# Sums of squares for the q and k norms from ScalarE's accumulator, head by head, instead of ScalarE's squares and VectorE's sums

## The chip, the cores and the metric

The kernel runs on one core of one Trainium2 chip. The metric is the device time in microseconds, as the median of several runs; lower is better.

## The reference, cut to what matters

A decoder trunk of two layers over 512 positions of width 1024, in float32. Layer 0 has an mLSTM group and a sparse-attention group (NSA: 8 query heads of 64 columns, 2 groups of keys and values); layer 1 is a gated linear recurrence (HGRN2). The change touches the norms and rotary turns of the NSA's queries, selected keys and window keys:

```python
def rms_norm(x, w):
    xf = x.astype(jnp.float32)
    return xf * lax.rsqrt(jnp.mean(xf * xf, axis=-1, keepdims=True) + EPS) * w.astype(jnp.float32)
...
    qh = partial_rope(rms_norm(heads(q, NSA_HEADS), q_norm), pos) * (d ** -0.5)
...
    ks_h = partial_rope(rms_norm(heads(ks, G), k_norm[1]), pos)
...
    kw_h = partial_rope(rms_norm(heads(kw, G), k_norm[2]), pos)
```

The mean runs over the 64 columns of one head, so a tile of 128 positions needs 8 sums for q, and 4 for k (2 groups, selected and window).

## The kernel before, in words

**Work.** All dense products run as three fp32r matmuls of a high and a low part. A weight tile comes in by DMA (`raw`), ScalarE rounds it (`whi`) and VectorE takes the rest (`wlo`). Layer 0 projects in groups: `cg` (compression inputs and gates), `nq` (queries), `nkv` (keys and values), `nz` (the gate z, called the z weights below), `mq`, `mk`, `mv`, `mo`, `mz`, then the output projection; layer 1 follows. A group's products go to PSUM buffers `mm`, and its evacuation on VectorE adds the bias and puts them in SBUF.

**The norms.** `nq_evac` and `nkv_evac` (lines 1175 to 1191) write the q and k columns of a 128-token tile to `qk` and start `prep_q(i)` or `prep_k(i)` (lines 1210 to 1269), once for each of the four tiles. A prep squares the tile on ScalarE into a buffer `sq`, multiplies the norm's weights in on GpSimd (`qk<-qk,qnB` or `knB`), sums the squares of each head on VectorE (`qss`, `kss`), takes the mean and the power -0.5 on GpSimd (`rsqrt_mean`, line 710: `qrs`, `krs`), multiplies on VectorE (`x<-qk,qrs` or `x<-qk,krs`), turns the first 16 columns (`rot`, three VectorE instructions with `r`), and lets TensorE transpose the result (`tp<-cs,x`). ScalarE and VectorE split the transposed tile into two parts (`q`, `kd`). With q of a tile and the compressed keys `kcd` the compressed scores follow (`sc<-kcd,q`, `ce`), and with all tiles of q and k the selected and window scores (`sc<-kd,q`).

**Beside it.** Between 30 and 55 us the gates of the mLSTM (`rows`, `ML`, `bd`) and the compressed keys (`gb`: a small product, a tanh on ScalarE that needs a table load, a transpose, another small product, giving `kr`, `kn`, `kh`, `kcd`) run beside the dense `nq` and `nkv` products.

**Order.** No engine's order is written out by hand. Generators (`Flow`) record the work, and a planner (`Plan.schedule`, lines 284 to 390) sets each engine's order from due times and from a price for each instruction (`price`, line 517); it is emitted at line 408, so nearly all instructions bear that line, and they are told apart by their tiles. Layer 0 and layer 1 are planned one after the other. Each engine then takes its queue in order. PSUM buffers for transposes (`tp`) are two, `mm` three; the raw weights have three buffers, the split ones four; the large scratch buffers `big` (which held `sq`) five.

ScalarE's accumulator is used in the kernel before too: by the mLSTM's head norms (`hj<-nd,rd`), by layer 1's (`hj<-tq`), by the compressed keys' norm (`kn<-kr`), and by the exponentials of the attention (`PP`). An instruction that reads the accumulator out, ACTIVATION_READ_ACCUMULATOR, stands behind each of them in the trace.

Of the kernel before, what the change touches and what calls it, by code (L numbers as in the profile page):

```python
# [16 lines left out]
AF = mybir.ActivationFunctionType  # L17
OP = mybir.AluOpType
AX = mybir.AxisListType
# [128 lines left out]
def cust(ap, dims, off=0):  # L148
    return bass.AP(tensor=ap.tensor, offset=ap.offset + off,
                   ap=[list(ap.ap[0])] + [list(d) for d in dims])  # L150
# [465 lines left out]
def build(tc, I, out):  # L616
    nc = tc.nc
    fl, pl = Flow(), Plan()
    V, A, P = (Paced(fl, e, n, pl) for e, n in ((nc.vector, "V"), (nc.scalar, "A"), (nc.gpsimd, "P")))
# [3 lines left out]
    with ExitStack() as ctx:  # L623
# [42 lines left out]
        def cut(t, shape, p=slice(0, 128)):  # L666
            n = 1
            for d in shape:
                n *= d
            v = t[p, :n]  # L670
            if len(shape) == 1:
                return v
            ls = "abcdef"[:len(shape)]
            return v.rearrange("p (" + " ".join(ls) + ") -> p " + " ".join(ls), **dict(zip(ls, shape)))
# [7 lines left out]
        def has(n):  # L682
            return lambda: room[0] >= n

        def u_t(name, shape, dt=F32):
            room[0] -= 1
            assert room[0] >= 0, name
            return cut(up.tile([128, 2064], dt, name=name, tag="u"), shape)

        def u_end(n):  # L690
            room[0] += n
# [18 lines left out]
        def rsqrt_mean(o, ss, n, inv, p=128):  # L710
            P.tensor_scalar(o, ss, inv, EPS, op0=OP.mult, op1=OP.add)
            P.tensor_tensor(o, o, hm[:p, :n], op=OP.pow)
# [234 lines left out]
        with ExitStack() as c0:  # L947
# [3 lines left out]
            def s_t(name, shape, bufs=2, dt=F32):  # L951
                return sp.tile(shape, dt, name=name, tag=name, bufs=bufs)
# [3 lines left out]
            def hb(n):  # L956
                return lambda: big[0] >= n

            def b_end(n=1):
                big[0] += n  # L960

            def b_t(name, shape, dt=F32):
                big[0] -= 1
                assert big[0] >= 0, name
                return cut(sp.tile([128, 1280], dt, name=name, tag="big", bufs=BB), shape)
# [24 lines left out]
            def E(n):  # L990
                return ev.setdefault(n, Mark())
# [183 lines left out]
            def nq_evac(i, p):  # L1175
                if i % 2 == 0:
                    t = u_t("qk", (2, 12, 64))
                    qk[i], qk[i + 1] = t[:, 0], t[:, 1]
                V.scalar_tensor_tensor(flat(qk[i][:, :8, :]), p, rs[:, i:i + 1], st["bq"], op0=OP.mult, op1=OP.add)
                fl.add(prep_q(i), 1)  # L1180


            def nkv_evac(i, p):
                if i == 0:
                    st["bk"] = bias_t("nkv", 512)
                    t = u_t("vp", (2, 1024))
                    st["vall"], st["pcT"] = cut(t[:, 0], (4, 4, 64)), cut(t[:, 1], (2, 512))
                bk = st["bk"]
                V.scalar_tensor_tensor(flat(qk[i][:, 8:, :]), p[:, :256], rs[:, i:i + 1], bk[:, :256], op0=OP.mult, op1=OP.add)
                V.scalar_tensor_tensor(flat(st["vall"][:, i]), p[:, 256:], rs[:, i:i + 1], bk[:, 256:], op0=OP.mult, op1=OP.add)  # L1190
                fl.add(prep_k(i), 1)
# [3 lines left out]
            def rot(x2, i):  # L1195
                r1 = s_t("r1", [128, 8, 16], 2)
                V.tensor_tensor(r1.rearrange("p a (c d) -> p a c d", c=2),
                                cust(x2, [[64, 8], [-8, 2], [1, 8]], 8),
                                cust(cs, [[0, 8], [8, 2], [1, 8]], SC["sin"] + 16 * i), op=OP.mult)
                V.tensor_tensor(x2[:, :, :16], x2[:, :, :16], cust(cs, [[0, 8], [1, 16]], SC["cos"] + 16 * i),  # L1200
                                op=OP.mult)
                V.tensor_tensor(x2[:, :, :16], x2[:, :, :16], r1, op=OP.add)

            def turn(x2):
                p = tp_t()
                for c in range(4):
                    T.transpose(p[:, 128 * c:128 * (c + 1)], flat(x2[:, 2 * c:2 * c + 2]), idf)
                return cut(p, (4, 128))

            def prep_q(i):  # L1210
                yield hb(2)
                x = qk[i][:, :8, :]
                ts_ = slice(128 * i, 128 * (i + 1))
                sq = b_t("sq", (8, 64))
                A.activation(sq, x, AF.Square)
                P.tensor_tensor(x, x, cust(qnB, [[0, 8], [1, 64]]), op=OP.mult)
                ss = s_t("qss", [128, 8])
                V.tensor_reduce(ss, sq, axis=AX.X, op=OP.add)
                b_end()
                rq = s_t("qrs", [128, 8])  # L1220
                rsqrt_mean(rq, ss, 8, 1.0 / 64)
                x2 = b_t("x2", (8, 64))
                V.tensor_tensor(x2, x, cust(rq, [[1, 8], [0, 64]]), op=OP.mult)
                rot(x2, i)
                yield [None, TPS, (lambda: q2) if i else has(2)]
                if i == 0:
                    q2.extend(u_t("q2", (2, 2, 512), F32R) for _ in range(2))
                p4 = turn(x2)
                b_end()
                for o in range(2):  # L1230
                    a, b = slice(64 * o, 64 * o + 64), slice(64 - 64 * o, 128 - 64 * o)
                    for g in range(2):
                        pg = p4[a, 2 * g:2 * g + 2]
                        A.activation(q2[g][a, o, :, ts_], pg, AF.Copy)
                        V.tensor_tensor(q2[g][b, o, :, ts_], pg, q2[g][a, o, :, ts_].bitcast(F32), op=OP.subtract)
                fl.mark(E("q%d" % i))
                fl.add(cmp_sm(i), 2)

            def prep_k(i):
                yield hb(2)  # L1240
                x = qk[i][:, 8:, :]
                ts_ = slice(128 * i, 128 * (i + 1))
                sq = b_t("sq", (4, 64))
                A.activation(sq, x, AF.Square)
                P.tensor_tensor(x.rearrange("p (a b) c -> p a b c", a=2), x.rearrange("p (a b) c -> p a b c", a=2),
                                cust(knB, [[64, 2], [0, 2], [1, 64]], 64), op=OP.mult)
                ss = s_t("kss4", [128, 4])
                V.tensor_reduce(ss, sq, axis=AX.X, op=OP.add)
                b_end()
                rk = s_t("krs4", [128, 4])  # L1250
                rsqrt_mean(rk, ss, 4, 1.0 / 64)
                x2 = b_t("x2", (8, 64))
                V.tensor_tensor(x2.rearrange("p (a b) c -> p a b c", a=4), cust(qk[i], [[64, 4], [0, 2], [1, 64]], 512),
                                cust(rk, [[1, 4], [0, 2], [0, 64]]), op=OP.mult)
                rot(x2, i)
                yield [None, TPS, (lambda: kd) if i else has(2)]
                if i == 0:
                    kd.extend(u_t("kd", (2, 2, 512), F32R) for _ in range(2))
                p4 = turn(x2)
                b_end()  # L1260
                for g in range(2):
                    pg = p4.rearrange("p (b g) t -> p g b t", b=2)[:, g]
                    A.activation(kd[g][:, 0, :, ts_], pg, AF.Copy)
                    V.tensor_tensor(kd[g][:, 1, :, ts_], pg, kd[g][:, 0, :, ts_].bitcast(F32), op=OP.subtract)
                fl.mark(E("k%d" % i))
                if i == 3:
                    u_end(2)
                    fl.add(nsa_a(), 0)
                    fl.add(nsa_b(), 0)
# [448 lines left out]
        with ExitStack() as c1:  # L1718
# [23 lines left out]
            for j in range(2):  # L1742
                a = s_t(f"AL{j}", [128, 4, 32], 1)
# [375 lines left out]
```

## Time and profile before

| | |
|---|---|
| runs | 623.8, 623.28, 620.89 us; median 623.28 |
| profiled execution | 619.54 us |
| its span, first to last instruction | 617.8 us |
| busy: TensorE, weight loads | 609.2 us (99%), 492.0 us (80%) |
| busy: VectorE, ScalarE, GpSimd | 463.9 us (75%), 326.4 us (53%), 104.5 us (17%) |
| mean granted TensorE clock | 0.997 of full |

The names are those of the profile: PE is TensorE's matmuls, PEld its weight loads, DVE VectorE, ACT ScalarE, POOL GpSimd, SP SyncE. Matmuls overlap one another, so the distance between two starts says what one costs, not its duration; the same holds for short ACT and DVE instructions. A busy PE may still run slower than it could.

### The profile page before, as it was taken

The numbers are of one execution on the slowest core, as the hardware profiler recorded it, in microseconds if no ns is written. First come the engines' busy times: TensorE is split into PE (matmuls) and PEld (weight loads), VectorE is DVE, ScalarE is ACT, GpSimd is POOL, SyncE is SP. The second block draws the span as 40 slices with busy tenths as digits, with TensorE's granted clock in tenths as the row PEclk, the third lists the DMA queues.
The fourth block names the chain that finished last, engine by engine and source line by source line (L and its number), as shares of the span: only waits on it lengthen the run. The fifth ranks groups of instructions, "written<-read, shape, count | busy, mean of one in ns | idle before, by whom it ended". The sixth has DMA issues, their size and how long they took to land.

```text
span 617.8 us, 11670 instructions
## 1 busy us (share of the span) xinstructions
PE 609.2 (99%) x4498; PEld 492.0 (80%) x4498; DVE 463.9 (75%) x988; ACT 326.4 (53%) x778; POOL 104.5 (17%) x131
## 2 busy tenths in 40 slices
PE   8999998999999999999999999999999999999997
PEld 8877886877777777888888887788877877788886
DVE  5888989988899875656746669997688798986441
ACT  7554433675676765273534757447527375565410
POOL 1424252031100000063003111023000100122100
PEclk9998999999999999999999999999999999999999
DMA  8823137679994004016244424473222215473111
GB/s 293 278 117 103 51 103 256 203 164 342 247 203 138 0 2 147 7 46 228 77 162 136 154 85 138 118 240 121 69 72 69 70 34 173 138 282 128 35 69 68
DMA packets 23526, 82.90 MB, mean 134 GB/s; under 512 B 3376, under 2 KB 4272, under 8 KB 20656
## 3 DMA queue, kind: packets, MB, share of 16 engines
q1 hardware_dynamic: 21168, 65.39, 32.2%
q0 software_dynamic: 2304, 16.78, 10.3%
q8 instruction: 35, 0.57, 0.4%
q14 instruction: 19, 0.16, 0.1%
HBM read 77.96 MB, written 20.97 MB: 160 GB/s over the span
## 4 chain that ended last, share of the span: by engine, by line
PE 92%; DVE 3%; DMA 1%; issue 1%; POOL 1%; ACT 1%; SPq 0%; ACTq 0%; DVEq 0%
PE mm L408 35%; PE mx L408 17%; PE my L408 15%; PE sc L408 8%; PE tp L408 5%; PE ac L408 5%; PE tq L408 5%; PE sd L408 2%; DMA raw<-in_wall_dram 1%; DVE wlo L408 1%; DVE HB L408 0%; DVE AL L408 0%; POOL krs L408 0%; ACT whi L408 0%; DVE x L408 0%
## 5 line engine op out<-in xcount | busy, mean ns | idle before, releaser
L408 ACT ACTIVATE whi<-raw 128x512 fp32r<-128x512 f32 (+1 forms) x184 | 105.0, 614 | 76.2 <-PE my L408 29.5
L408 DVE TENSOR_TENSOR wlo<-raw,whi 128x1024 fp32r<-128x1024 f32 (+1 forms) x96 | 114.7, 1202 | 20.4 <-ACT whi L408 20.1
L408 PE MATMUL mm<-whi,h0h 128*128 128x512 f32 (+1 forms) x168 | 68.2, 407 | 0.0
L408 PE MATMUL mm<-whi,h0l 128*128 128x512 f32 (+1 forms) x168 | 67.9, 405 | 0.0
L408 PE MATMUL mm<-wlo,h0h 128*128 128x512 f32 (+1 forms) x168 | 67.4, 405 | 0.0
L408 ACT ACTIVATE PP<-sc,nm 128x128 f32<-128x128 f32 (+2 forms) x64 | 33.7, 527 | 26.0 <-DVE nm L408 22.9
L408 DVE CUSTOM_DVE_ANT_0 sc<-sc,cz 128x128 f32<-128x128 f32 (+2 forms) x64 | 31.4, 502 | 11.7 <-PE sc L408 9.1
L408 PE MATMUL mm<-h0h,whi 128*128 128x512 f32 x96 | 39.5, 411 | 0.0
L408 PE MATMUL mm<-h0h,wlo 128*128 128x512 f32 x96 | 38.1, 397 | 0.6 <-DVE wlo L408 0.6
L408 PE MATMUL mm<-h0l,whi 128*128 128x512 f32 x96 | 38.6, 402 | 0.0
L408 PEld LDWEIGHTS mm<-whi,h0l 128*128 128x128 f32 x168 | 32.1, 192 | 5.8 <-issue 0.2
L408 PEld LDWEIGHTS mm<-wlo,h0h 128*128 128x128 f32 x168 | 32.2, 192 | 5.6 <-issue 0.2
L408 PEld LDWEIGHTS mm<-whi,h0h 128*128 128x128 f32 x168 | 32.3, 192 | 5.2
L408 DVE TENSOR_TENSOR HB<-HB,tt 128x512 f32<-128x512 f32 x48 | 31.9, 687 | 4.4 <-PE sd L408 3.1
L408 PE MATMUL sc<-kd,q 128*128 128x512 f32 (+3 forms) x128 | 31.3, 330 | 0.0
L408 ACT ACTIVATE PT<-tp 128x384 f32<-128x384 f32 (+1 forms) x48 | 24.0, 526 | 9.5 <-PE tp L408 9.2
L408 POOL TENSOR_TENSOR ivgg<-ivgg,zz 128x256 f32<-128x256 f32 x16 | 17.8, 1116 | 65.9 <-ACT zz L408 65.9
L408 POOL TENSOR_SCALAR hr<-hs 128x4 f32<-128x4 f32 x12 | 2.3, 193 | 142.7 <-ACT hj L408 142.6
L408 PE MATMUL tp<-cs,PP 128*128 128x128 f32 x160 | 26.3, 275 | 0.0
L408 PEld LDWEIGHTS sc<-kd,q 128*128 128x128 f32 x128 | 22.7, 191 | 4.0 <-ACT PT L408 0.8
L408 PE MATMUL my<-h1l,whi 128*128 128x512 f32 x64 | 25.8, 403 | 0.0
L408 PE MATMUL mx<-h1l,whi 128*128 128x512 f32 x64 | 25.8, 402 | 0.0
(374 smaller groups left out, 1556.7 us busy)
## 6 DMA issues: line engine op xcount, KB each, us to landing
raw<-in_wall_dram SPq DMA_DIRECT2D x76, 512.0 KB, 3.8
wt<-in_wall_dram POOLq DMA_DIRECT2D x12, 1024.0 KB, 14.2
raw<-wt SPq DMA_DIRECT2D x16, 512.0 KB, 3.7
wt<-wt POOLq DMA_DIRECT2D x4, 1024.0 KB, 22.7
bias<-in_brow_dram SPq DMA_DIRECT2D x9, 256.0 KB, 4.1
xt<-in_xt_dram SPq DMA_DIRECT2D x8, 256.0 KB, 5.4
w<-in_cw_dram SPq DMA_DIRECT2D x2, 1024.0 KB, 9.4
x<-in_xt_dram SPq DMA_DIRECT2D x2, 1024.0 KB, 6.8
```

Of the source, the lines that this page charges most:

```text
L408: o.fn(*o.a, **k)
```

## The change

A helper `squares` calls one ScalarE activation for each head, with 64 columns in and a scratch tile out, and lets the accumulator write the head's sum. The buffer `sq`, the full-width square and VectorE's `tensor_reduce` go, and a prep waits for one large scratch buffer instead of two. What follows, from `rsqrt_mean` on, is the same code.

```diff
+            def squares(x, ss):
+
+                j = cut(s_t("sqj", [128, 512], 1), (8, 64))
+                for a in range(x.shape[1]):
+                    A.activation(j[:, a, :], x[:, a, :], AF.Square, accum_out=ss[:, a:a + 1])
+
             def prep_q(i):
-                yield hb(2)
+                yield hb(1)
                 x = qk[i][:, :8, :]
                 ts_ = slice(128 * i, 128 * (i + 1))
-                sq = b_t("sq", (8, 64))
-                A.activation(sq, x, AF.Square)
+                ss = s_t("qss", [128, 8])
+                squares(x, ss)
                 P.tensor_tensor(x, x, cust(qnB, [[0, 8], [1, 64]]), op=OP.mult)
-                ss = s_t("qss", [128, 8])
-                V.tensor_reduce(ss, sq, axis=AX.X, op=OP.add)
-                b_end()
...
             def prep_k(i):
-                yield hb(2)
+                yield hb(1)
                 x = qk[i][:, 8:, :]
                 ts_ = slice(128 * i, 128 * (i + 1))
-                sq = b_t("sq", (4, 64))
-                A.activation(sq, x, AF.Square)
+                ss = s_t("kss4", [128, 4])
+                squares(x, ss)
...
-                ss = s_t("kss4", [128, 4])
-                V.tensor_reduce(ss, sq, axis=AX.X, op=OP.add)
-                b_end()
```

The planner then sets another order for the first layer. Two places of it matter. The first is ScalarE's queue around the table load for the tanh of the compressed keys (`gb`); `cT` are the compression inputs, `qk_174` holds q tiles 0 and 1. Before:

```order
L408 ACTIVATE cT_152<-tp_157 64x64x8
L408 ACTIVATE sq_175<-qk_174 128x512
L408 ACT_TABLE_LOAD
L408 ACTIVATE gb_161<-gb_161 128x128
L408 ACTIVATE whi_180<-raw_170 128x512 x2
L408 ACTIVATE gb_161<-tp_173 128x64
L408 ACTIVATE sq_182<-qk_174 128x512
```

With the change:

```order
L408 ACTIVATE cT_152<-tp_157 64x64x8
L408 ACTIVATE sqj_176,qss_175<-qk_174 128x64 x8
L408 ACTIVATE sqj_183,qss_182<-qk_174 128x64 x8
L408 ACT_TABLE_LOAD
L408 ACTIVATE gb_161<-gb_161 128x128
L408 ACTIVATE gb_161<-tp_173 128x64
L408 ACTIVATE whi_180<-raw_170 128x512 x2
```

The squares of both tiles now stand ahead of the table load, and the first weight split has moved behind `gb`.

The second is VectorE's queue at the last two splits of the z weights: `wlo_260` and `wlo_268` before, `wlo_263` and `wlo_271` with the change; `x2_264` and `x2_267` are k tile 2. Before:

```order
L408 SCALAR_TENSOR_TENSOR vp_232<-mm_249,rs0_89,bias_231 128x256
L408 TENSOR_REDUCE kss4_262<-sq_261 128x4
L408 TENSOR_TENSOR wlo_260<-raw_230,whi_259 128x1024
L408 SCALAR_TENSOR_TENSOR qk_206<-mm_251,rs0_89,bias_231 128x256
L408 TENSOR_TENSOR x2_264<-qk_206,krs4_263 128x512
L408 TENSOR_TENSOR wlo_268<-raw_266,whi_267 128x1024
L408 TENSOR_REDUCE kss4_270<-sq_269 128x4
L408 TENSOR_TENSOR r1_265<-x2_264,cs_68 128x128
L408 TENSOR_TENSOR x2_264<-x2_264,cs_68 128x8x16
L408 TENSOR_TENSOR x2_264<-x2_264,r1_265 128x8x16
L408 TENSOR_TENSOR kd_275<-tp_277,kd_275 128x2x128
```

With the change:

```order
L408 SCALAR_TENSOR_TENSOR qk_205<-mm_250,rs0_89,bias_230 128x256
L408 SCALAR_TENSOR_TENSOR vp_231<-mm_250,rs0_89,bias_230 128x256
L408 TENSOR_TENSOR wlo_263<-raw_225,whi_262 128x1024
L408 TENSOR_TENSOR wlo_271<-raw_269,whi_270 128x1024
L408 TENSOR_REDUCE ce_256<-sc_255 128x256
L408 TENSOR_TENSOR x2_267<-qk_205,krs4_266 128x512
L408 TENSOR_REDUCE mx8_257<-ce_256 128x8
L408 SCALAR_TENSOR_TENSOR qk_205<-mm_251,rs0_89,bias_230 128x256
L408 TENSOR_TENSOR ce_256<-ce_256,mx8_257 128x256
L408 TENSOR_TENSOR r1_268<-x2_267,cs_68 128x128
L408 TENSOR_TENSOR x2_267<-x2_267,cs_68 128x8x16
```

Both weight splits have moved ahead of the multiplication of k tile 2, and work on the compressed scores (`ce`, `mx8`) of an earlier tile stands between the steps of k tile 2.

## Rows read from the trace of the kernel before

**Rows 1.** The page, part 1: busy time, share of the span, instructions.
```profile
PE 609.2 (99%) x4498; PEld 492.0 (80%) x4498; DVE 463.9 (75%) x988; ACT 326.4 (53%) x778; POOL 104.5 (17%) x131
```
**Rows 2.** Windows: length, busy of PE, PEld, DVE, ACT, POOL; PE clock, DMA share, GB/s.
```profile
80.00:100.00 20.00, 18.16 (x91) 14.34 (x90) 17.94 (x40) 6.14 (x16) 8.22 (x11) 1.00 0.57 196
```
**Rows 3.** Timeline of PE around 94 us: start, duration, engine, what, [idle before, releaser].
```profile
92.83 0.40 PE L408 MATMUL mm<-h0h,whi 128*128 128x512 f32 x1
93.07 0.39 PE L408 MATMUL mm<-h0l,whi 128*128 128x512 f32 x1
94.05 0.50 PE L408 MATMUL mm<-h0h,wlo 128*128 128x512 f32 x1 [0.59 <-DVE wlo L408]
94.39 0.39 PE L408 MATMUL mm<-h0h,whi 128*128 128x512 f32 x1
95.99 0.63 PE L408 MATMUL tp<-cs,x 128*128 128x128 f32 x4 [1.21 <-DVE kd L408]
```
**Rows 4.** Timeline of DVE in the same stretch.
```profile
91.40 0.69 DVE L408 TENSOR_TENSOR x<-qk,krs 128x512 f32<-128x512 f32 x1 [1.48 <-POOL qk L408]
92.01 1.98 DVE L408 TENSOR_TENSOR wlo<-raw,whi 128x1024 fp32r<-128x1024 f32 x1
...
95.09 0.75 DVE L408 TENSOR_TENSOR kd<-tp,kd 128x256 fp32r<-128x256 f32 x2
```
**Rows 5.** Windows of 4 us around the fall of the clock, columns as in rows 2.
```profile
48.00:52.00 4.00, 4.00 (x14) 2.86 (x15) 3.22 (x14) 1.16 (x3) 0.98 (x2) 0.82 0.00 2
52.00:56.00 4.00, 4.00 (x16) 2.98 (x16) 3.60 (x5) 1.18 (x4) 1.25 (x2) 0.76 0.52 158
```
**Rows 6.** Instructions on tile sq: durations min/median/max in ns, starts, forms.
```profile
L408 ACT ACTIVATE sq<-qk x8: 409/520/632, 37.3 to 90.0; 128x512 f32<-128x512 f32 x4, 128x256 f32<-128x256 f32 x4
L408 DVE TENSOR_REDUCE qss<-sq x4: 668/676/680, 42.4 to 64.5; 128x8 f32<-128x512 f32 x4
L408 DVE TENSOR_REDUCE kss<-sq x4: 405/412/420, 76.9 to 93.9; 128x4 f32<-128x256 f32 x4
```
**Rows 7.** Timeline of ACT where the accumulator is used, three places.
```profile
47.65 0.26 ACT L408 ACTIVATE kn<-kr 64x64 f32<-64x64 f32 x1 [1.20 <-DVE kr L408]
47.82 0.19 ACT L408 ACTIVATION_READ_ACCUMULATOR kn<-kr 64x1 f32 x1
...
107.75 0.19 ACT L408 ACTIVATION_READ_ACCUMULATOR PP<-sc,nm 128x1 f32 x1
107.87 0.48 ACT L408 ACTIVATE PP<-sc,nm 128x256 f32<-128x256 f32 x1
...
262.10 0.39 ACT L408 ACTIVATE hj<-nd,rd 128x128 f32<-128x128 f32 x1
...
262.61 0.40 ACT L408 ACTIVATE hj<-nd,rd 128x128 f32<-128x128 f32 x1
```
**Rows 8.** Timeline of ACT, 34 to 43 us.
```profile
34.69 1.28 ACT L408 ACT_TABLE_LOAD   x1
35.99 0.31 ACT L408 ACTIVATE ef<-ef,cs 128x16 f32<-128x16 f32 x1
...
37.32 0.63 ACT L408 ACTIVATE sq<-qk 128x512 f32<-128x512 f32 x1 [0.54 <-DVE qk L408]
37.97 1.28 ACT L408 ACT_TABLE_LOAD   x1
42.50 0.31 ACT L408 ACTIVATE gb<-gb 128x128 f32<-128x128 f32 x1 [3.25 <-DVE gb L408]
```
**Rows 9.** Timeline of DVE and of PE where the tanh is taken up.
```profile
44.52 0.25 DVE L408 SCALAR_TENSOR_TENSOR gb<-gb 128x128 f32<-128x128 f32 x1
...
44.91 0.30 PE L408 MATMUL tp<-cs,gb 128*128 128x128 f32 x1
```
**Rows 10.** Timeline of POOL: mean and power of a q tile, weights of the next.
```profile
60.37 1.64 POOL L408 TENSOR_TENSOR qrs<-qrs,hm 128x8 f32<-128x8 f32 x1
61.97 1.29 POOL L408 TENSOR_TENSOR qk<-qk,qnB 128x512 f32<-128x512 f32 x1
```

## The prediction

> **What bounds the kernel now.** I read the page first. TensorE (PE) is busy for 99% of the span and VectorE (DVE) for 75%, ScalarE (ACT) for 53% [rows 1]: no work that is taken off DVE shortens anything unless PE stands still for it somewhere, so the question is where PE waits. The changed code runs once for each of four 128-token tiles of q and of k, from 37 to 95 us. I therefore cut that stretch into windows. In 80 to 100 us DVE is busy for 17.94 of 20 us, ACT for 6.14, and PE for 18.16 only [rows 2]. The timeline of PE shows where the missing time lies: dense matmuls of 512 columns start 0.24 us apart (92.83 to 93.07); then one starts 0.98 us after the one ahead (93.07 to 94.05, waiting for a DVE `wlo`), and the transposes of k tile 2 start 1.60 us after the matmul ahead (94.39 to 95.99, waiting for a DVE `kd`) [rows 3]. Over the pace that is 0.74 + 1.36 = 2.1 us.
>
> On DVE the reader sees why. The `wlo` at 92.01 is the low part of the fourth z weight; it is queued behind an `x<-qk,krs` that itself stood 1.48 us for GpSimd (POOL), and the `kd` at 95.09 comes after both [rows 4]. So the 2.1 us come from DVE's queue and from the norm chain of k tile 2. One more loss lies in the stretch: in 48 to 56 us the granted clock is 0.82 and then 0.76, that is, part of each window at 1.2 instead of 2.4 GHz, behind some 5 us in which single fp32 transposes and tiny matmuls alternate with dense ones. It costs 0.18 x 4 + 0.24 x 4 = 1.7 us [rows 5].
>
> **The change part by part.** *Removed:* on DVE four sums of 0.676 us (q) and four of 0.412 us (k), 4.35 us in all; on ACT eight squares, 8 x 0.520 = 4.2 us [rows 6]. All of the DVE work except the last 0.41 us stands ahead of the stall at 95.99.
>
> *Added:* 48 ACT squares of 64 columns, each followed by an instruction that reads the accumulator. The trace has no group of them at this size that runs without waits. The nearest row in size is the one of the compressed keys (64 columns from SBUF): its read starts 0.17 us after it. After a read, the next activation starts 0.12 us later where it does not wait for the same scratch buffer (107.75 to 107.87). That makes 0.29 us. Where every call writes one scratch tile and takes a scale operand, the distance is 0.51 us (262.10 to 262.61) [rows 7]. In the new order only the first of each eight (or four) waits, and the calls write different columns, so I take 0.29 and keep 0.51 as the upper end; the lower end is 0.17, if the read hid altogether. ACT then gets 48 x 0.29 = 13.9 us, 9.7 us more than before, spread over some 58 us in which it is mostly idle (6.14 of 20 us in [rows 2]).
>
> The Trainium skill, page "ScalarE: Activation LUTs", section "What ACT_TABLE_LOAD costs", speaks against splitting work so: an ACTIVATE with immediates costs 186 ns plus 0.833 ns per element, whatever its size, with some 93 ns of overlap back to back. For 64 columns that would be an estimated 0.146 us each, 7.0 us for 48, and the late ScalarE below would have no chance at all. The rows add the accumulator read to that [rows 7], so it keeps one.
>
> *First place, the gates and compressed keys (37 to 45 us).* ACT's queue now holds the sixteen squares of q tiles 0 and 1, then the table load, then the tanh `gb`. Before, one square started at 37.32, the load (1.28 us) ran at 37.97, and the tanh at 42.50 waited for DVE [rows 8]. Now the squares end at 37.32 + 16 x 0.29 = 42.0, the load at 43.2, the tanh at 43.6: 0.7 us later than before. DVE took that result at 44.52 and PE its transpose at 44.91 [rows 9]. DVE loses one 0.68 us sum ahead of that point and gets four tiny instructions of 0.15 us pulled ahead of it, so it would again come there at about 44.5. The tanh is hidden with 0.9 us to spare: cost 0. With 0.51 the squares end at 45.5, the tanh at 47.1, and PE stands 47.1 - 44.5 = 2.6 us.
>
> That page also states, in the same section, that a table load is followed by a drain of 1.38 us; that would bring the tanh to an estimated 45.0 and cost 0.4 us. Here the activation behind a load started 0.02 us after the load's end (34.69 + 1.28, then 35.99) [rows 8], so I go by the row.
>
> *DVE's x of q tile 1* now stands directly behind that of tile 0. POOL has to multiply (1.29 us) and raise to a power (1.64 us) for each tile, one tile after the other [rows 10]: with tile 0's sums at 37.32 + 8 x 0.29 = 39.6, POOL ends tile 0 at about 42.8 and tile 1 at about 46.0 (with 0.2 us each for the scaling). DVE comes there at about 47, where it took tile 0's x before. Cost 0; were POOL 1 us slower, the two weight splits queued behind that x would be late next, and they are asked for only after 56 us.
>
> *Third place, the z weights (84 to 96 us).* DVE's new order puts the last two z `wlo` directly behind k tile 1's evacuations and ahead of `x<-qk,krs` of k tile 2. So the 0.74 us wait goes, unless the weight splits come later than 93.3, and DVE has up to 3.9 us less to do by then. PE's transposes of k tile 2 now stand after 8 more dense matmuls, 8 x 0.24 = 1.9 us later; the work of the compressed scores that was pulled ahead on DVE uses up some of what was freed. So the 1.36 us go between wholly and not at all. I take 1.0 of them: it is nearer to "wholly", because the 1.48 us for which DVE stood for POOL no longer delay anything PE waits for at once.
>
> *The rest:* the same matmuls, the same DMAs, the same weight splits. PE's sequence up to the fall of the clock differs only by three q matmuls that are issued a few places later during the load of the inputs, where PE waits for data anyway, so I leave the fall in. Before layer 0's output projection begins, every engine's order is the one of before again, so that projection and layer 1 cost what they did.
>
> *Sum:* 0.7 + 1.0 = 1.7 us off. The profiled execution took 619.54 us (span 617.8 and 1.7 around it), so it would come to 617.8. It stood 3.7 us below the median of the runs shown (623.28, from 620.89 to 623.8); the same 1.7 us off the median makes **621.6 us**, 0.3% less. A measurement of this kernel can tell about 0.5%, 3.1 us, from no change.
>
> **The rivals.**
> - *Also the clock.* ACT and DVE timing around 45 us shifts, and the fall at 50 us does not come: another 1.7 us, 619.9. For it: the fall came during a stretch of scattered work whose spacing DVE and ACT partly set. Against it: PE's sequence there is unchanged.
> - *Hidden anyway.* DVE's freed time is eaten by waits on POOL, which this change does not relieve (the 1.48 us in [rows 4] is such a wait), or a new gap of the same size opens at another of the eight transposes: 623.3.
> - *ScalarE comes late: slower.* The code that sets the order prices a square with its accumulator at 0.234 us. At 0.51 each group of eight is 2.2 us later than planned, and PE, which takes its queue in order, stands for it: 2.6 us at the tanh, and 2.2 us at one of the two later q tiles, with the old 2.1 us staying: 623.3 + 4.8 = 628.1. It decides from about 0.35 us per square on (0.29 plus the 0.9 us of room over 16). For it: rows at 0.51 exist. Against: they wait for a shared scratch tile, which these do not.
>
> **How the numbers follow.** Chances: the forecast 0.56, also the clock 0.12, hidden anyway 0.19, ScalarE late 0.13. Faster by over 0.5%: the 0.12, and 0.06 of the forecast's case where both stalls and small waits go: 0.18. Slower: 0.13. The rest is the same: 0.69. The range leaves out most of the slow rival and a thin tail below: its low end is the clock's case with the whole 2.1 us and another 1.3 us of scatter (618.2), its high end the wait at the tanh alone, with nothing gained (623.3 + 2.6 = 625.9).
>
> **What would show it.** Right: eight DVE sums gone; squares about 0.29 us apart; ACT up by 9 to 10 us in 37 to 95; PE busy over 19 of 20 us in 80 to 100, with no wait for `wlo` there; window 48 to 56 at the same clock; layer 1 as long as before. Wrong: a wait of PE for the tanh's transpose near 45 us or for an `x` over 1 us; distances of 0.4 us or more between squares; a second fall of the clock; or layer 1 longer by itself.

## The result and the profile after

The change makes the kernel slower: 623.75 us median against 619.96 of the kernel before (21 runs each), ratio 1.0059 with a 95% interval from 1.0046 to 1.0072. The prediction was a gain of 0.3%, so even its sign is wrong. The 623.28 us that it started from was the median of three runs; over 21 runs the kernel before takes 3.3 us less. The profiled execution took 625.16 us, with a span of 623.4 against 617.8.

**Page part 1 after**, against [rows 1]:

```profile
PE 609.8 (98%) x4498; PEld 492.0 (79%) x4498; DVE 456.2 (73%) x980; ACT 333.2 (53%) x866; POOL 104.2 (17%) x131
```

DVE has 8 instructions and 7.7 us less, ACT 6.8 us more; PE's busy time grew by 0.6 us while the span grew by 5.6, so PE stands and waits more. **Windows after**, columns as in [rows 2] and [rows 5]:

```profile
52.00:56.00 4.00, 4.00 (x22) 3.25 (x20) 1.74 (x6) 1.41 (x3) 0.60 (x2) 1.00 0.56 181
66.00:70.00 4.00, 3.63 (x12) 3.06 (x13) 3.34 (x8) 0.42 (x1) 1.81 (x2) 0.57 0.00 0
80.00:100.00 20.00, 19.31 (x99) 15.83 (x98) 18.29 (x47) 10.12 (x37) 8.26 (x11) 1.00 0.54 175
140.00:160.00 20.00, 17.03 (x83) 12.39 (x82) 13.11 (x31) 9.60 (x23) 2.44 (x3) 0.96 1.02 272
158.00:162.00 4.00, 3.92 (x11) 3.13 (x12) 4.00 (x14) 2.39 (x7) 0.00 (x0) 0.57 1.02 255
```

In 80 to 100 us PE is busy for 1.15 us longer than in [rows 2]. The fall of the clock at 50 us [rows 5] is not there; two others are, in 66 to 70 and in 158 to 162 us, each 0.43 x 4 = 1.7 us. And in 140 to 160 us PE is busy for 17.03 us. **The same window before**:

```profile
140.00:160.00 20.00, 20.00 (x106) 15.44 (x105) 17.28 (x41) 13.53 (x33) 2.45 (x3) 1.00 1.02 315
```

Three waits in **PE's timeline after** are new (the rows stand at 66, 100 and 158 us); the first two stand at transposes of the normed tiles (`tp<-cs,x`), and the largest is outside the stretch in which the changed code runs:

```profile
66.37 0.47 PE L408 MATMUL tp<-cs,x 128*128 128x128 f32 x1 [1.12 <-DVE x L408]
...
100.02 0.33 PE L408 MATMUL tp<-cs,x 128*128 128x128 f32 x1 [0.71 <-ACT vp L408]
...
158.08 0.51 PE L408 MATMUL sc<-kd,q 128*128 128x256 f32 x2 [2.97 <-ACT PP L408]
```

What stands behind the 2.97 us is read from **the chain of work that ended last, after, 139.95 to 158.08 us** (start, duration, what). In the kernel before, the chain of this stretch is PE alone.

```profile
139.95 1.11 DVE wlo L408
...
141.09 11.70 DMA raw<-in_wall_dram
...
152.87 0.07 ACT whi L408
...
154.06 1.23 DVE wlo L408
155.28 0.66 DVE cva L408
155.94 0.60 DVE mq L408
156.55 0.61 DVE sc L408
...
157.25 0.79 ACT PP L408 x2
...
158.08 0.51 PE sc L408 x2
```

A raw weight tile of 512 KB is asked for at 141.09 us, when a `wlo` gives its buffer back, and takes 11.70 us to land. ACT and DVE come to it early, and each takes its queue in order: the `whi` and `wlo` of that weight hold up the `cva`, `mq`, score and exponential instructions behind them, and PE runs out of work. **ACT's timeline after** shows the place:

```profile
146.33 0.49 ACT L408 ACTIVATE PT<-tp 128x384 f32<-128x384 f32 x1
152.87 1.15 ACT L408 ACTIVATE whi<-raw 128x512 fp32r<-128x512 f32 x2 [6.05 <-DMA raw<-in_wall_dram]
...
157.25 0.69 ACT L408 ACTIVATE PP<-sc,nm 128x512 f32<-128x512 f32 x1 [2.00 <-DVE nm L408]
```

The load is slow because the DMA is full (share 1.02 in the window above). POOL issues sixteen DMAs, `presums` in the code, that add pairs of layer 1's weight blocks in DRAM (`wt<-in_wall_dram`, `wt<-wt`, 1 MB each). **POOL's timeline after:** seven of them go out in one burst, as soon as POOL is done with a `th`:

```profile
119.33 0.62 POOL L408 TENSOR_SCALAR th<-th 128x512 f32<-128x512 f32 x1 [3.59 <-ACT th L408]
119.89 4.37 POOL L408 DMA_DIRECT2D wt<-in_wall_dram  x7
```

**Before**, the load was slow too. The DMA issues between 141 and 142 us (KB, median us to landing) hold one load:

```profile
raw<-in_wall_dram SPq DMA_DIRECT2D x1, 512.0 KB, 9.6
```

POOL's burst and ACT's use of that load, on their timelines before:

```profile
126.05 4.11 POOL L408 DMA_DIRECT2D wt<-in_wall_dram  x6
```

```profile
150.74 1.15 ACT L408 ACTIVATE whi<-raw 128x512 fp32r<-128x512 f32 x2 [0.35 <-PE mm L408]
```

It was asked for at 141.08, landed 9.6 us later at 150.7, and ACT came to it at 150.74: just in time, which nothing in the waits of the kernel before shows. After the change the burst is 6 us earlier and has one sum more, the load lands 2.1 us later (11.7 against 9.6), and ACT comes to it 3.6 us earlier (free at 146.8; before at 150.4). It does not queue behind the sums, it shares the DMA with them. **DMA issues after, 136 to 137 us:**

```profile
wt<-wt POOLq DMA_DIRECT2D x1, 1024.0 KB, 25.4
```

This sum, issued at 136.85, lands at 162.2, 9 us after the load that was issued behind it. The Trainium skill, page "DMA: Bandwidth & Descriptors", section "Queues, rings and completion order", says that each DMA engine takes turns between its queues packet by packet. This row agrees in so far as the later load lands first; the turns themselves stand in no row.

### The profile page after: what moved, and what is told of

Read it like the earlier page. It is cut to its first block, busy times and chain, and to the rows that moved or that the text cites. A ratio compares the mean times of both kernels' runs of the same rounds, so it can differ in the third digit from the quotient of the medians.

```text
span 623.4 us, 11764 instructions
## 1 busy us (share of the span) xinstructions
PE 609.8 (98%) x4498; PEld 492.0 (79%) x4498; DVE 456.2 (73%) x980; ACT 333.2 (53%) x866; POOL 104.2 (17%) x131
## 4 chain that ended last, share of the span: by engine, by line
PE 84%; DVE 6%; DMA 3%; ACT 3%; issue 1%; POOL 1%; SPq 0%; DVEq 0%; ACTq 0%
PE mm L408 29%; PE mx L408 18%; PE my L408 15%; PE sc L408 6%; PE tq L408 5%; PE tp L408 5%; PE ac L408 4%; DMA raw<-in_wall_dram 3%; PE sd L408 2%; DVE wlo L408 1%; DVE x L408 1%; ACT whi L408 1%; POOL qk L408 1%; DVE q L408 1%; DVE ce L408 0%
## 5 line engine op out<-in xcount | busy, mean ns | idle before, releaser
L408 DVE TENSOR_TENSOR wlo<-raw,whi 128x1024 fp32r<-128x1024 f32 (+1 forms) x96 | 113.4, 1187 | 34.7 <-ACT whi L408 30.4
L408 PE MATMUL sc<-kd,q 128*128 128x128 f32 (+3 forms) x128 | 31.8, 332 | 3.0 <-ACT PP L408 3.0
L408 PE MATMUL mx<-h1h,wlo 128*128 128x512 f32 x64 | 25.7, 402 | 0.1
```

The lines of the kernel that those rows point to most:

```text
L408: o.fn(*o.a, **k)
```

## The experiments

Theory: the operations of the change are worth what the prediction says or more, and the planner's new order costs more than that; its main loss is the load above. Rival: the operations cost it (6.8 us more on ACT, a longer chain for each norm). Ratios are to the kernel before.

**1 and 2. Order and operations apart.** The planner gets the prices and dependences of one kernel, and at emission the operations of the other stand in their places. Order of before, operations of the change (likewise for k):

```diff
                 A.activation(sq, x, AF.Square)
+                ss = s_t("qss", [128, 8])
+                pl.ops[-1].fn = heads(sq, x, ss)
                 P.tensor_tensor(x, x, cust(qnB, [[0, 8], [1, 64]]), op=OP.mult)
-                ss = s_t("qss", [128, 8])
                 V.tensor_reduce(ss, sq, axis=AX.X, op=OP.add)
+                pl.ops[-1].fn = nothing
```

> The order of the kernel before with the operations of the change: the planner still sees one Square and one sum by VectorE; where it put the Square, the 8 or 4 accumulating activations are emitted, and where it put the sum, nothing. Theory (the new order costs the 3.7 us, the operations nothing): ratio to before 0.995 to 1.001, no wait of ScalarE for a weight load at about 150 us, no 3 us gap of TensorE at about 158 us. Rival (the operations cost it, ScalarE's 0.24 us per head against 0.64 us for a whole square of q, 6.8 us more work in all): ratio 1.004 to 1.008, with TensorE waiting for ScalarE or for the longer chain of the norms between 40 and 100 us.

Order of the change, operations of before:

```diff
                 for a in range(n):
                     A.activation(j[:, a, :], x[:, a, :], AF.Square, accum_out=ss[:, a:a + 1])
+                    pl.ops[-1].fn = lambda *a, **k: None
+                pl.ops[-n].fn = lambda *a, **k: nc.scalar.activation(j[:, :n, :], x, AF.Square)
+                pl.ops[-1].fn = lambda *a, **k: nc.vector.tensor_reduce(ss, j[:, :n, :], axis=AX.X, op=OP.add)
```

> The order of the change with the operations of the kernel before: the planner sees the 8 or 4 accumulating activations; at the first of them the whole Square is emitted, at the last the sum by VectorE, and nothing between. Theory (order): ratio to before 1.003 to 1.007, and the wait of ScalarE for a weight load at about 147 to 153 us with the gap of TensorE near 158 us is there again. Rival (operations): ratio 0.997 to 1.002, since ScalarE has its 6.8 us back.

Measured:

| | squares and VectorE sums | accumulator, head by head |
|---|---|---|
| order of before | 1 (619.7 us) | 617.74 us, 0.9967 (0.9955 to 0.9980) |
| order of the change | 626.06 us, 1.0110 (1.0086 to 1.0133) | 623.75 us, 1.0059 (1.0046 to 1.0072) |

Down the columns, the order costs 1.1% and 0.9%; along the rows, the operations gain 0.3% and 0.5%. In the run with the new order and the old operations, VectorE's sums stand where the planner had the last activation, a place that was not set for them, so the 0.5% is the less certain of the two. The rival falls: the same operations gain 2.0 us in the old order. **With the old order and the new operations** (window, then PE's timeline) PE in 80 to 100 us has most of the 1.84 us back that it lacked in [rows 2], and of the two waits of [rows 3] only 0.40 us is left:

```profile
80.00:100.00 20.00, 19.60 (x100) 16.13 (x99) 17.38 (x40) 8.30 (x32) 7.02 (x9) 1.00 0.60 209
```

```profile
92.92 0.39 PE L408 MATMUL mm<-h0h,whi 128*128 128x512 f32 x1
93.71 0.63 PE L408 MATMUL tp<-cs,x 128*128 128x128 f32 x4 [0.40 <-DVE kd L408]
```

**With the new order and the old operations** the chain of the result is there again (waits in 140 to 165 us: total, times, longest):

```profile
ACT whi L408 <- DMA raw<-in_wall_dram: 6.5, 1, 6.5
...
PE sc L408 <- ACT PP L408: 3.4, 1, 3.4
```

**3 and 4. One half of the change each.** The new `prep_q` with the old `prep_k`, and the reverse.

```diff
-                A.activation(sq, x, AF.Square)
+                squares(x, ss)
...
-                V.tensor_reduce(ss, sq, axis=AX.X, op=OP.add)
```

> The change in the preparation of q alone (32 of the 48 activations). Theory (order): the planner makes a third order, so the time is its own and no share of the change's: anywhere from 0.995 to 1.008, with gaps of TensorE at places where neither kernel has them. Rival (operations): two thirds of the change's loss, ratio 1.003 to 1.005.

> The change in the preparation of k alone (16 of the 48 activations). Theory (order): a fourth order, anywhere from 0.995 to 1.008, and the losses of q alone and k alone don't add up to that of the change. Rival (operations): one third of the loss, ratio 1.001 to 1.003, and the two add up to 1.006.

Measured: q alone 618.17 us, 0.9965 (0.9950 to 0.9981); k alone 624.12 us, 1.0068 (1.0046 to 1.0089). Two thirds of the new operations gain 0.35%, one third loses 0.68%: the time follows the order that comes out, not the amount changed. The run with k alone has the wait of the result (waits in 140 to 165 us); the one with q alone has PE busy for all of 140 to 160 us. Its three loads issued between 140 and 149 us are as slow (median 15.2 us), but ACT never waits for one of them: it is the early use, and not the slow load by itself, that costs.

```profile
ACT whi L408 <- DMA raw<-in_wall_dram: 5.3, 1, 5.3
...
PE tp L408 <- ACT PT L408: 3.6, 1, 3.6
```

**5 and 6. The sums held back.** The change with its order of PE, ACT and DVE, but the last ten sums wait behind a POOL copy of one column of the last `mk`; and the kernel before with the same.

```diff
+        held = [o for o in order if o.eng == "P" and "_ns" in o.k][6:]
         for o in order:
+            if o in held:
+                continue
...
+            if o is gate and held:
+                self.pool.tensor_copy(self.gate, o.a[0][:, :1])
+                for h in held:
+                    h.fn(*h.a, **{n: v for n, v in h.k.items() if n != "_ns"})
```

> The change, every order the same on every engine but POOL's: the last ten of the sixteen sums of weights are issued behind a small POOL copy that reads the last mk, at about 205 to 215 us, so that the weight loads issued at 141 to 155 us have the DMA to themselves. Theory (the loss is a weight load that shares the DMA with the sums and holds up ScalarE's and VectorE's queues): the load of 141.09 us lands in under 5 us, ScalarE doesn't wait at 147 us, the 3.14 us gap of TensorE at 158 us is gone and with it the fall of the clock behind it; 3 to 5 us less than the change, ratio to before 0.997 to 1.002. Rival (the loss is spread over the new order, or made by ScalarE's added work): still 1.004 to 1.007.

> The control: the kernel before with the same ten sums held back. Its order puts the squared weights' first use later, so its load was just in time (landed at 150.66, used at 150.74). Theory: no change, ratio 0.997 to 1.002. Rival (holding the sums back is worth something by itself, by the DMA's load on other engines): 0.990 to 0.996.

Measured: 625.93 us, 1.0077 (1.0048 to 1.0105), and 624.38 us, 1.0057 (1.0036 to 1.0078). Both totals miss what was expected, though the wait in question is gone: the load of the change lands in 3.6 us. But the ten sums now begin at 220 us (217 in the control), and the next weight loads, asked for from 236 us on, are the slow ones. **Waits of the change with ten sums held, 240 to 256 us:**

```profile
ACT whi L413 <- DMA raw<-in_wall_dram: 7.9, 1, 7.9
...
PE sc L413 <- ACT E L413: 3.8, 1, 3.8
```

The clock falls right behind this wait too (0.61 in 250 to 254 us), and the control loses the same way, with a wait of 2.1 us in the same stretch. So these two runs show that such a collision costs as much at another place (4.2 us in the control, which had none), and don't yet show what the change loses without it.

**7 and 8. The planner told of slow loads.** Loads planned between 145 and 195 us take longer in the plan.

```diff
-                xfer = max(xfer, t + 1125.0) + x.k["_ns"]
-                x.done = xfer
+                busy = 145000.0 < t < 195000.0
+                xfer = max(xfer, t + 1125.0) + (max(x.k["_ns"], 6200.0) if busy else x.k["_ns"])
+                x.done = xfer + (5000.0 if busy else 0.0)
```

> The change, with a planner that is told of the slow loads: a load planned between 145 and 195 us (planned time, some 18 us ahead of the chip's there) takes 6.2 us of the transfer and lands 5 us later. The order is the change's up to about the load; behind it the split of the weights stands later in ScalarE's and VectorE's queues, behind the attention's scores. Theory: the gap at 158 us shrinks below 1 us, ratio to before 0.997 to 1.002. Rival: 1.004 to 1.007.

> The control: the kernel before with the planner told the same. There is no wait for that load to be removed, so theory: 0.997 to 1.003, and rival (the order about 150 us is worth several us by itself in either kernel): 0.990 to 0.996.

Measured: 625.09 us, 1.0065 (1.0044 to 1.0087), and 619.80 us, 0.9990 (0.9970 to 1.0009). The control came as expected; the change did not get better. ACT still waits 6.3 us for the load, and PE 3.2 us behind it: in the order that came out, the split of that weight still stands ahead of the same exponentials. Why the planner kept it there was not tested. The window was set by the expectation's estimate that the plan runs some 18 us off the chip there, which no run shows, so it stays open whether the plan was told of this load at all, and the run says nothing for or against the theory.

**9 and 10. The sums held back in two parts,** five behind the third `mq`, five behind the third `mk`, so that they run between the weight loads; and the kernel before with the same.

```diff
+        gates = {mq[2]: held[:5], mk[2]: held[5:]} if held else {}
...
+            if o in gates:
+                self.pool.tensor_copy(self.gate, o.a[0][:, :1])
+                for h in gates[o]:
+                    h.fn(*h.a, **{n: v for n, v in h.k.items() if n != "_ns"})
```

> The change with its orders kept, as with all ten sums held back, but in two parts, each behind a POOL copy of one column: five sums behind the third mq (at about 154 us, when the loads issued at 140 to 148 us have landed), five behind the third mk (about 201 us), so that they are through before the weight loads of 236 us on, which were slow in the run with all ten behind the last mk. Theory: no gap of TensorE over 1 us at 158 us nor at 249 us; 3 to 5 us less than the change, ratio to before 0.996 to 1.002; what stays of the new order are the gaps at 66 and 99 us, some 2.5 us together against the 2.1 us that before has at 94 to 96 us. Rival (the loss moves to wherever the order is tight): a gap of 2 us or more elsewhere and 1.004 to 1.008.

> The control: the kernel before with its ten sums held back in the same two parts. It has no wait for these loads, so 0.997 to 1.002.

Measured: 619.86 us, 0.9991 (0.9973 to 1.0009), and 619.87 us, 1.0000 (0.9984 to 1.0017). The change is 3.9 us faster than without this, as expected, and the kernel before is not. Without the collision the change is level with the kernel before. **The change with the sums in two parts,** the three loads issued between 140 and 149 us (DMA issues: KB, median us to landing):

```profile
raw<-in_wall_dram SPq DMA_DIRECT2D x3, 512.0 KB, 3.3
```

ACT and PE in the place of the wait, on their timelines:

```profile
146.79 1.16 ACT L414 ACTIVATE whi<-raw 128x512 fp32r<-128x512 f32 x2
```

```profile
154.79 0.39 PE L414 MATMUL mm<-h0h,whi 128*128 128x512 f32 x1
155.02 0.40 PE L414 MATMUL sc<-kd,q 128*128 128x256 f32 x2
```

ACT's `whi` stands where it stood, and waits for nothing; PE's `sc<-kd,q` starts 0.23 us after the matmul ahead, where it stood for 2.97. What is left against the 617.74 us of experiment 1 are the two smaller waits of the new order; they are there in this run too (waits in 60 to 104 us):

```profile
PE tp L414 <- DVE x L414: 1.1, 1, 1.1
PE tp L414 <- ACT vp L414: 1.1, 1, 1.1
```

**11 and 12. Another order, no other work.** One constant of the planner's due times, in the change and in the kernel before.

```diff
-WU, MARGIN, SLACK = 9, 0, 1.5
+WU, MARGIN, SLACK = 9, 0, 1.4
```

> The change with another constant in the planner (SLACK 1.4 for 1.5), which changes no work and makes another order. Theory (the order alone moves the time by some us either way): its own time, 0.990 to 1.012, with gaps of TensorE at other places than the change's. Rival (the change itself costs 0.6%): 1.004 to 1.008.

> The kernel before with the same constant (SLACK 1.4), no work changed. Theory: an order of its own, 0.990 to 1.012, and over 0.3% from before in one direction or the other. Rival (orders are worth little, the operations decide): 0.998 to 1.002.

Measured: 634.03 us, 1.0219 (1.0188 to 1.0249), and 630.21 us, 1.0160 (1.0130 to 1.0191). Both lie beyond the spread that was expected, on the slow side. A constant that changes no work moves the kernel before by 10 us. Not all of that was followed; in both, layer 1 has a new wait (**the kernel before with the other constant, 385 to 400 us**):

```profile
PE mx L408 <- DVE ivgg L408: 4.7, 1, 4.7
```

**A version that beats both** is experiment 1, 617.74 us, 0.33% below the kernel before with an interval that excludes no gain: the change's operations in the order that the old prices make. The change in q alone (experiment 3, 0.35%) is level with it.

## Why the prediction was wrong

- *The number came near by luck.* The measured 623.75 us lies inside the range (618.2 to 625.9), but only because the prediction started 3.3 us too high, from three runs; it forecast 1.7 us less than the kernel before, and the runs show 3.8 us more.
- *What bounds the kernel: right.* The two waits at 94 to 96 us went, 0.7 + 1.0 us off in the forecast's sum. With the order held as it was, the operations gave 2.0 us (1.2 to 2.8 by the interval), against the 1.7 of that sum. One reading was off without effect: the last 0.41 us sum, which the prediction leaves behind the stall at 95.99, ran at 93.9 [rows 6], ahead of it.
- *Third place and sum, the first step that failed.* In the planner's new order the two waits went too, but the sum has no term for new ones, and two came, 1.12 us at 66 us for an `x` (of the kind that the prediction lists as a sign of being wrong) and 0.71 us at 100 us for `vp`: 1.8 us for the 2.1 us that went. With the old operations in this order both are there again (1.0 and 1.2 us), so they are the order's. That is the prediction's rival "hidden anyway", by its second condition, a new gap at another transpose; experiment 9, which has these waits and not the collision, comes out at its "nothing gained" (0.9991).
- *A square with its accumulator, taken as 0.29 us, measured 0.24.* This and the two rows below are **ACT's timeline after**:

```profile
37.90 0.24 ACT L408 ACTIVATE sqj<-qk 128x64 f32<-128x64 f32 x1
38.05 0.19 ACT L408 ACTIVATION_READ_ACCUMULATOR sqj<-qk 128x1 f32 x1
38.14 0.24 ACT L408 ACTIVATE sqj<-qk 128x64 f32<-128x64 f32 x1
...
41.74 1.28 ACT L408 ACT_TABLE_LOAD   x1
43.03 0.31 ACT L408 ACTIVATE gb<-gb 128x128 f32<-128x128 f32 x1
```

  The distance of the starts, 37.90 to 38.14, lies between the lower end (0.17) and the value taken; the read starts 0.15 us behind its activation and takes 0.09 more of the distance. So 48 cost 48 x 0.24 = 11.5 us. The estimate of 7.0 us from the Trainium skill, page "ScalarE: Activation LUTs", section "What ACT_TABLE_LOAD costs", fits the distance to the read and leaves the read out.
- *First place, cost 0: right.* The tanh ran from 43.03 to 43.34 (its end was put at 43.6 in the prediction). DVE took its result up at 45.04 only (44.5 in the prediction), and PE's transpose started 0.54 us after the matmul ahead, 0.32 before: 0.2 us, and not the tanh's. The drain of 1.38 us behind a table load that the same section of the Trainium skill states would have put its start at an estimated 44.4; it started 0.01 us after the load's end.
- *ScalarE comes late: this rival gave the right sign by the wrong mechanism.* Its condition, 0.35 us or more per square, is not met.
- *The rest, the step that failed most.* The prediction says of the rest "the same matmuls, the same DMAs, the same weight splits", and puts it at nothing; it has no term for the stretch between the norms and layer 0's output projection, where the order also differs (a third place, beside the two that the section on the change names). The amount of work is the same; the distance between a load's landing and its first use is not. The 3 us at 158 us come from there, and experiments 9 and 10 show it: with that load in time the change is 3.9 us faster. For layer 1, where the order is the old one again, the prediction is right: from layer 1's first matmul to the end of the span it is 270.8 us before and 271.8 after, and the order of before takes 271.6 in experiment 1, so the 1.0 us is not the change's. **First matmul group of layer 1, before, after and in experiment 1** (starts, first and last):

```profile
L408 PE MATMUL mx<-h1h,whi x64: 387/394/500, 347.0 to 508.0; 128*128 128x512 f32 x64
...
L408 PE MATMUL mx<-h1h,whi x64: 387/394/500, 351.6 to 513.5; 128*128 128x512 f32 x64
...
L408 PE MATMUL mx<-h1h,whi x64: 387/394/507, 344.7 to 506.3; 128*128 128x512 f32 x64
```

- *The clock.* The fall at 50 us stayed in the forecast; in the profiled execution it went and two others came, each beside a new wait of PE, 1.7 us more. The fall at 50 us is not tied to either order: in 48 to 56 us the kernel before with the sums in two parts (experiment 10) has 1.00, the change with them (experiment 9) 0.79. The mean granted clock of the kernel before lies between 0.991 and 1.000 from execution to execution, so not much should rest on the clock's part of the sum below.
- *The sum of the profiled executions.* Up to layer 1 the change is 4.6 us late (347.0 against 351.6). New: 3.0 + 1.1 + 0.7 us of waits and 1.7 us of clock; gone: 2.1 us. That is 4.4 of the 4.6 us; with the 1.0 us in layer 1 it is 5.4 of the 5.6 us by which the span grew. PE's wait of 0.86 us for a `whi` at 8.86 us is new as well but no loss: before, the same matmul started at 9.12 us.

## What to carry to other kernels

Where a planner or scheduler writes the order, an edit is two changes, its operations and a new order, and the second can be the larger: hold the order (emit the new operations in the old places) before judging an edit, and measure how far another order alone moves the time. A load that lands just as it is wanted shows up in no list of waits: compare each landing with its first use, and most of all where another queue fills the DMA. On engines that take their queue in order, a weight split that stands early holds up everything behind it when its load is late.

## What the runs showed of the hardware

- A weight load of 512 KB lands in 3.3 us when no sum is in flight (median of three, experiment 9). Beside the 1 MB sums the one issued at 141 us takes 9.6 us before and 11.7 us after, and the three issued after between 140 and 149 us have a median of 14.1 us (**DMA issues after**; 12.2 before). A full DMA share (1.02) was there in both kernels and said nothing about which one would wait.

```profile
raw<-in_wall_dram SPq DMA_DIRECT2D x3, 512.0 KB, 14.1
```

- Eight accumulating activations in a row that write different columns run 0.24 us apart, with the read of the accumulator inside that distance.
